# Seven-product FFN pairs that go on adding to sums already read, with a new step order, in a two-layer grid diffusion block on one core

## The chip, the cores and the metric

The kernel runs on one core of a Trainium2 chip. The metric is the device time of one launch in microseconds (us). Inputs and outputs are fp32; TensorE is fed with fp32r operands, and nearly every fp32 product is made of three passes over a high and a low part of each factor, which all add into one PSUM sum.

## The reference

Two layers work on 512 latent tokens and 256 context tokens of width 1024. A layer normalizes and modulates the tokens, projects them, runs four mixers (neighbourhood attention, a gated linear recurrence, retention, differential attention), projects back with `w_out`, and then runs the gated feed-forward part (FFN) on which the change works. The second layer does the FFN on the latent tokens alone:

```python
def swiglu(h, w1, w2):
    g, u = jnp.split(h @ w1, 2, axis=-1)
    return (jax.nn.silu(g) * u) @ w2

h2 = modulate(rms_norm(xl_mid, g_pre_ffn[l]), mod_l[3], mod_l[4])
xl_new = xl_mid + mod_l[5] * rms_norm(swiglu(h2, w_ffn_in[l], w_ffn_out[l]), g_post_ffn[l])
```

`w1` has 2 x 2816 columns: 22 blocks of 128 columns for `g`, and as many for `u`. One block of `g` with the block of `u` that belongs to it is called a pair here.

## The kernel before

Nothing is issued where it is written. Class `Issue` records every operation; its `run` (from line 373) then goes through a list schedule with cost and latency tables, and issues the instructions of each engine in that order, from one line, L573. So all rows of the profile name line 573, and instructions are told apart by tiles: `T` (128 x 1024, 26 of them), `t` (128 x 512, six), `D` (128 x 3072, seven), `st` (small columns), and in PSUM `a` (four of 512 columns) and `s` (two of 1024). What decides the order: the order in which the program is recorded (`ORDER`, a string of letters per layer that says which mixer takes the next step, d, n, l, r, and m for the modulation weights), how far ahead of the oldest open operation a buffer may be taken (`AHEAD`, one number for each of seven stages), a bias between VectorE and ScalarE for operations that either can do (`BIAS`), and limits on the `T` tiles that each use may hold (`LIMIT`). The queues themselves run in order: an instruction that waits holds all behind it on its engine.

The seven stages follow each other with small overlaps: start with the first modulation vectors; mixers of layer 1; `w_out` and FFN pairs of layer 1; the FFN's output product of layer 1; mixers of layer 2; `w_out` and the 22 pairs of layer 2; the output product of layer 2 (`ffn_out8`).

A pair of the second layer is computed in one of two ways. With the halves of the model width and the halves of the tokens it is a 2 x 2 by 2 x 2 block product. `ffn_pair8` (line 1690) makes the eight products of that directly: per product 4 x 3 matmuls of 128 x 128 by 256 columns, 96 in all. `ffn_pair` (line 1629) makes seven (a Strassen-Winograd scheme): 84 matmuls, but more sums on VectorE (DVE), before the products on the weights and after them on the results. The list `CLASSIC` (line 587) names the pairs of each layer that take eight products: in the second layer 0, 1, 2, 14, 18 and 21. In `ffn_pair` each of the seven products has a PSUM region of its own, and the results are put together in `t` tiles.

Other tables that the change touches: `WCH` says in which chunks the eight blocks of `w_out` are taken, for the first and the second half of the tokens; `RES` how many of its split weights stay in SBUF between the halves (two in layer 1, seven in layer 2); `OUT8` how the 22 blocks of `ffn_out8` are grouped; `FIRST` which projection weights are loaded early, among the modulation weights of the start (`prefetch`: index i of the list is loaded with quarter i).

Of the kernel before, what the change touches and what calls it, by code (L numbers as in the profile page):

```python
# [13 lines left out]
AF = mybir.ActivationFunctionType  # L14
ALU = mybir.AluOpType
# [7 lines left out]
NF = DFF // 128  # L23
# [148 lines left out]
class Issue:  # L172
# [7 lines left out]
        def __getattr__(self, fn):  # L180
            return lambda *a, **k: self.q.add(self.name, fn, a, k)

    AHEAD = (10 ** 9, 183, 161, 90, 339, 135, 40)
    LOCK = 1
    BIAS = (100, 800, 500, 0, 200, 300, 200)

    def __init__(self, nc):
        self.real, self.ops, self.tags, self.kinds = nc, [], {}, {}
# [387 lines left out]
class Net:  # L576
# [13 lines left out]
    FIRST = ((3, 0), (7, 0))  # L590
    ORDER = ("drlmddlllrddrrnllrdrmrddrmdrlmrrmmdrdrmdlndmmmddnnnmdmnnnmmdndnnnnnmnnrmnn",
             "dlllldlrdlldrdddrdrrrddrdldnrdnnnnnnnrnrrndnnnrn")

    LIMIT = dict(r=(2, 61, 57, 4, 1, 19, 3), m=(14, 4, 6, 33, 8, 28, 5), wh=(7, 58, 35, 12, 28, 42, 5), fw=(4, 68, 77, 14, 43, 48, 9), fa=(38, 3, 10, 19, 23, 13, 9), W=(20, 43, 11, 9, 28, 32, 41), wo=(97, 51, 25, 30, 33, 17, 9))

    def __init__(self, tc, I, out, ND=7):
        self.tc, self.nc, self.I, self.out = tc, Issue(tc.nc), I, out
# [978 lines left out]
    def ffn_in_T(self, l, halves, ctx, out):  # L1576


        nc = self.nc
        H = 128 * len(halves[0])  # L1580
# [12 lines left out]
        for t, ids in enumerate(halves):  # L1593
            xs = yield
            ns = [self.normed(xs[i]) for i in ids]
            for c in range(0, 8, cpt):
# [16 lines left out]
                nm = "12"[c // 4] + "12"[t]  # L1613
                if nm in names:
                    split(nm, q[t, c], c % 4)
        for c in range(0, 4, cpt):
            b11, b21, b12, b22 = q[0, c], q[0, c + 4], q[1, c], q[1, c + 4]
            t3 = self.T()[:, 0:cpt * H]
            self.sub(t3, b22, b12)
            self.sub(b12, b12, b11)  # L1620
            split("T1", b12, c)
            self.sub(b22, b22, b12)
            split("T2", b22, c)
            self.sub(b21, b22, b21)
            split("T4", b21, c)
            split("T3", t3, c)
        yield

    def ffn_pair(self, l, f, B, dst):
# [57 lines left out]
        nc.scalar.activation(s, s, AF.Silu)  # L1687
        self.tt(dst[:, H:n], s, c22, ALU.mult)

    def ffn_pair8(self, l, f, B, dst):  # L1690

        nc = self.nc
        n = dst.shape[1]
        H = n // 2
        A = [self.split_w(self.raw_in(self.I["w_ffn_in"][l, i])) for i in (f, NF + f)]
        for t in range(2):
            ps = self.S()
            g, u = (ps[:, i * 512:i * 512 + H] for i in range(2))
            for out, (wh, wl) in zip((g, u), A):
                for k in range(8):  # L1700
                    bh, bl = (B["12"[k // 4] + "12"[t], w][:, k % 4 * H:(k % 4 + 1) * H] for w in "hl")
                    c = slice(k * 128, k * 128 + 128)
                    self.mm3(out, wh[:, c], wl[:, c], bh, bl, k == 0, k == 7)
            s = nc.buf("t")[:, 0:H]
            nc.scalar.activation(s, g, AF.Silu)
            nc.vector.tensor_tensor(dst[:, t * H:(t + 1) * H], s, u, ALU.mult)
            if t == 0:
                yield

    def ffn(self, l, B, ctx, order):  # L1710
# [7 lines left out]
        for i, f in enumerate(seq):  # L1718
            if ctx:
                dst[f] = (self.W() if i < NF - self.KEEP else self.T())[:, 0:n]  # L1720
            else:
# [375 lines left out]
```

## Time and profile before

| | |
|---|---|
| median of 3 runs | 1703.21 us (1701.01 to 1704.25) |
| the profiled execution | 1701.83 us |
| its span, first to last instruction | 1700.0 us |
| busy: TensorE, its weight loads, DVE, ScalarE, GpSimd | 96%, 84%, 73%, 49%, 10% |
| mean granted clock of TensorE | 0.982 of full speed |

The profile shows for each engine when it was busy and what ended its idle time; PE is TensorE, PEld its weight loads, ACT is ScalarE, POOL is GpSimd, SP is the engine whose queue starts the transfers. A clock of 1.00 is the 2.4 GHz level, 0.50 the 1.2 GHz level. Instructions of one engine overlap a little at their ends, so that the distance from start to start is a better price for one of a row of them than its own length.

### The profile page before, as it was taken

What the parts mean: (1) busy time and instruction counts of PE and PEld (TensorE: products, weight loads), DVE (VectorE), ACT (ScalarE), POOL (GpSimd) and SP (SyncE); (2) the same over time, 40 slices, a digit from 0 to 9 for tenths busy, and PEclk for the clock granted to TensorE, in tenths of its full rate; (3) what the DMA queues carried; (4) which work ended last, traced back from release to release, by engine and by line L of the source; (5) the groups of instructions that cost most, each with busy time, mean ns of one, the idle gap of its engine ahead of it and who ended that gap; (6) DMA issues with size and microseconds to landing.
All of it is one profiled execution on the core that took longest, in us unless ns stands there. A gap on an engine that the chain in (4) does not pass through costs nothing. (4 is left out here: it accounts for less than half of the span.)

```text
span 1700.0 us, 26804 instructions
## 1 busy us (share of the span) xinstructions
PE 1638.9 (96%) x10487; PEld 1420.5 (84%) x10487; DVE 1248.2 (73%) x2133; ACT 831.3 (49%) x1388; POOL 161.8 (10%) x152
## 2 busy tenths in 40 slices
PE   7998999999999999999999889999999999999998
PEld 4887778677869999999987678889877899999886
DVE  5686656848589877887689998888656799886442
ACT  4366734767564333343343475765555544443221
POOL 1010100000111011001001220022120000100000
PEclk8999999999999999999999989999989999999999
DMA  9342467657573232233955551532134422332332
GB/s 377 115 149 62 162 226 260 214 182 260 187 257 136 69 112 93 101 104 108 313 174 195 207 197 57 186 130 79 38 118 149 173 83 92 112 99 89 118 129 75
DMA packets 81617, 254.64 MB, mean 150 GB/s; under 512 B 8661, under 2 KB 14133, under 8 KB 81489
## 3 DMA queue, kind: packets, MB, share of 16 engines
q1 hardware_dynamic: 81224, 252.81, 42.8%
q8 instruction: 82, 1.34, 0.3%
q14 instruction: 47, 0.38, 0.1%
q10 hardware_dynamic: 264, 0.11, 0.0%
HBM read 224.80 MB, written 28.08 MB: 149 GB/s over the span
## 5 line engine op out<-in xcount | busy, mean ns | idle before, releaser
L573 ACT ACT_TABLE_LOAD x30 | 38.5, 1283 | 7.2 <-issue 2.6
L573 PE MATMUL a<-D_0u,T_21u 128*128 128x384 f32 (+2 forms) x88 | 27.4, 340 | 0.0
L573 PE MATMUL a<-D_0u,T_12u 128*128 128x256 f32 (+2 forms) x84 | 26.4, 337 | 0.0
L573 PE MATMUL a<-D_0u,T_25u 128*128 128x256 f32 (+2 forms) x68 | 23.5, 346 | 0.0
L573 PE MATMUL a<-D_0u,T_1u 128*128 128x256 f32 (+2 forms) x76 | 22.5, 334 | 0.0
L573 PE MATMUL a<-D_0u,T_18u 128*128 128x256 f32 (+2 forms) x64 | 19.4, 335 | 0.1
L573 PE MATMUL s<-D_6u,D_4u 128*128 128x512 f32 (+1 forms) x66 | 17.9, 355 | 1.4 <-issue 1.1
L573 PE MATMUL s<-D_4u,D_5u 128*128 128x512 f32 (+1 forms) x66 | 17.8, 358 | 1.1 <-ACT T_17u L573 0.6
L573 PEld LDWEIGHTS a<-D_0u,T_21u 128*128 128x128 f32 x88 | 16.5, 190 | 2.1 <-DVE T_16u L573 0.9
L573 ACT COPY t_4u<-s 128x384 f32<-128x384 f32 (+1 forms) x16 | 6.9, 430 | 22.2 <-PE s L573 22.1
L573 PE MATMUL a<-D_2u,T_25u 128*128 128x512 f32 (+1 forms) x52 | 17.7, 341 | 0.0
L573 DVE TENSOR_TENSOR st_6u<-st_6u 128x1 f32<-128x1 f32 x1 | 0.2, 159 | 23.7 <-ACT T_15u L573 23.7
L573 PEld LDWEIGHTS s<-D_6u,D_4u 128*128 128x128 f32 x66 | 11.0, 188 | 7.7 <-ACT T_18u L573 1.7
L573 PE MATMUL a<-D_3u,T_12u 128*128 128x384 f32 (+2 forms) x52 | 16.9, 351 | 0.0
L573 ACT COPY t_5u<-s 128x384 f32<-128x384 f32 (+1 forms) x12 | 5.2, 434 | 23.3 <-PE s L573 23.3
L573 PEld LDWEIGHTS a<-D_0u,T_12u 128*128 128x128 f32 x84 | 15.6, 188 | 1.1
L573 PE MATMUL a<-D_0u,T_22u 128*128 128x256 f32 (+2 forms) x48 | 15.0, 328 | 1.6 <-ACT T_25u L573 1.6
L573 PE MATMUL a<-D_3u,T_1u 128*128 128x512 f32 (+2 forms) x52 | 16.4, 341 | 0.0
L573 ACT ACTIVATE t_1u<-t_1u 128x384 f32<-128x384 f32 (+1 forms) x17 | 8.2, 480 | 16.8 <-DVE t_1u L573 16.8
L573 PEld LDWEIGHTS a<-D_0u,T_25u 128*128 128x128 f32 x68 | 12.9, 190 | 4.0 <-issue 1.9
L573 PE MATMUL a<-D_2u,T_12u 128*128 128x256 f32 (+1 forms) x48 | 16.1, 336 | 0.0
L573 PE MATMUL a<-D_3u,T_25u 128*128 128x512 f32 (+2 forms) x48 | 15.8, 342 | 0.0
(4134 smaller groups left out, 6625.5 us busy)
## 6 DMA issues: line engine op xcount, KB each, us to landing
D_4u<-dstk SPq DMA_DIRECT2D x12, 384.0 KB
T_7u<-in_w_mod_dram SPq DMA_DIRECT2D x8, 512.0 KB
T_6u<-in_w_mod_dram SPq DMA_DIRECT2D x7, 512.0 KB
T_20u<-in_w_mod_dram SPq DMA_DIRECT2D x7, 512.0 KB
T_22u<-in_w_in_dram SPq DMA_DIRECT2D x7, 512.0 KB
T_24u<-in_w_mod_dram SPq DMA_DIRECT2D x6, 512.0 KB
T_1u<-in_w_in_dram SPq DMA_DIRECT2D x6, 512.0 KB
D_6u<-dstk SPq DMA_DIRECT2D x8, 384.0 KB
```

The source lines that it names most:

```text
L573: getattr(getattr(self.real, op.eng), fn)(*map(real, a), **{x: real(v) for x, v in k.items()})
```

## The change

Three things change.

First, a new function `ffn_pair_sums` takes the place of `ffn_pair` in the second layer. It makes seven products as well, with 84 matmuls, but in three PSUM tiles x, y and z: a product is read out by a copy or a sum, and the next product is added to what the tile holds (`start=False`), so that sums which DVE made before are made in PSUM. The block T4 of the activations gets the other sign for this. Per pair, DVE's or GpSimd's sums of 128 x 256 go from nine to five, copies out of PSUM from two to three.

Second, pairs 14, 18 and 21 of the second layer go from eight products to seven; 0, 1 and 2 stay at eight.

Third, the tables get new values: `AHEAD`, `BIAS`, `LIMIT`, `ORDER`, `FIRST`, `EARLY`/`FILL`, `WCH`, `RES`, `OUT8`. `FILL` 4 in the place of 22 moves nothing: the four steps that are left to it are taken with pairs 0 to 3 in both. `RES` 1 and 4 means one more load and split of a `w_out` block in layer 1 and three more in layer 2.

```diff
-    AHEAD = (10 ** 9, 183, 161, 90, 339, 135, 40)
+    AHEAD = (703, 192, 161, 90, 368, 120, 10)
-    BIAS = (100, 800, 500, 0, 200, 300, 200)
+    BIAS = (50, 500, 500, 200, 200, 500, 300)
...
-    WCH = (((3, 2, 1, 1, 1), (3, 1, 1, 3)), ((4, 4), (1, 1, 2, 4)))
-    RES = (2, 7)
+    WCH = (((3, 2, 1, 1, 1), (3, 1, 1, 3)), ((5, 3), (4, 4)))
+    RES = (1, 4)
...
-    CLASSIC = ((), (0, 1, 2, 14, 18, 21))
-    OUT8 = (3, 2, 2, 2, 2, 2, 2, 2, 2, 3)
+    CLASSIC = ((), (0, 1, 2))
+    OUT8 = (2, 4, 3, 2, 2, 1, 2, 3, 3)
-    FIRST = ((3, 0), (7, 0))
+    FIRST = ((9, 0),)
...
+        x, y, z = (self.A()[:, 0:H] for _ in range(3))
+        c11, c12, c22 = (nc.buf("t")[:, 0:H] for _ in range(3))
+        product(x, "11", "11")
+        product(y, "12", "21")
+        self.copy(c11, x)
+        add(c11, c11, y, ALU.add)
+        nc.scalar.activation(c11, c11, AF.Silu)
+        yield
...
+        product(x, "S2", "T2", False)
+        self.copy(c12, x)
+        product(z, "S1", "T1")
+        self.copy(c22, z)
+        product(x, "S3", "T3", False)
+        add(c22, c22, x, ALU.add)
+        product(z, "S4", "22", False)
+        add(c12, c12, z, ALU.add)
+        nc.scalar.activation(c12, c12, AF.Silu)
+        self.tt(dst[:, H:n], c12, c22, ALU.mult)
+        product(x, "22", "T4", False)
+        add(dst[:, 0:H], c11, x, ALU.mult)
...
+        seven = self.ffn_pair if ctx else self.ffn_pair_sums
+        jobs = [(self.ffn_pair8 if i in self.CLASSIC[l] else seven)(l, f, B, dst[f]) for i, f in enumerate(seq)]
```

What this does to the order shows at three places.

DVE, in the middle of the second layer's pairs, before, from the operations around one pair to those of the next (`a` and `s` are PSUM results, 512 and 1024 wide rows prepare the weights of a later pair):

```order
L573 TENSOR_TENSOR t_2u_13380<-t_2u_13380,s_81 128x256
L573 TENSOR_TENSOR T_11u_13348<-T_11u_13348 128x512
L573 TENSOR_TENSOR T_20u_13482<-T_13u_13353,T_9u_13464 128x1024
L573 TENSOR_TENSOR t_1u_13498<-t_2u_13380,a_76 128x256
L573 TENSOR_TENSOR T_22u_13503<-T_11u_13348,T_15u_13487 128x1024
L573 TENSOR_TENSOR t_2u_13380<-t_2u_13380,t_5u_13477 128x256
L573 TENSOR_TENSOR T_13u_13518<-T_10u_13445,T_17u_13458 128x1024
L573 TENSOR_TENSOR t_5u_13477<-t_5u_13477,t_1u_13498 128x256
L573 TENSOR_TENSOR t_0u_13535<-T_14u_13451 128x512
L573 TENSOR_TENSOR t_1u_13498<-t_1u_13498,a_78 128x256
L573 TENSOR_TENSOR t_2u_13380<-t_2u_13380,a_77 128x256
```

The same place now, one whole pair:

```order
L573 TENSOR_TENSOR T_9u_13466<-T_24u_13358,T_22u_13431 128x1024
L573 TENSOR_TENSOR t_1u_13473<-t_1u_13473,a_77 128x256
L573 TENSOR_TENSOR t_3u_13452<-t_3u_13452,a_78 128x256
L573 TENSOR_TENSOR T_24u_13519<-T_1u_13475,T_19u_13503 128x1024
L573 TENSOR_TENSOR T_5u_13524<-t_3u_13452,t_1u_13473 128x256
L573 TENSOR_TENSOR T_5u_13524<-t_0u_13415,a_77 128x256
L573 TENSOR_TENSOR t_4u_13533<-T_11u_13480 128x512
L573 TENSOR_TENSOR T_11u_13480<-T_1u_13475,T_11u_13480 128x512
L573 TENSOR_TENSOR T_7u_13552<-t_4u_13533,T_4u_13544 128x512
L573 TENSOR_TENSOR t_5u_13538<-t_5u_13538,a_79 128x256
L573 TENSOR_TENSOR T_1u_13475<-t_4u_13533,T_1u_13475 128x512
L573 TENSOR_TENSOR T_1u_13475<-T_1u_13475 128x512
```

The third 1024 wide subtraction of the pair has gone to GpSimd: in the stage of `w_out` and pairs of the second layer GpSimd now has 21 of that width, four before.

ACT, near the end of the second layer's mixers, before: casts of mixer results that come back from DRAM (`D<-T`), among copies of PSUM tiles that the attention's matmuls wait for:

```order
L573 COPY T_25u_11557<-s_81 128x1024
L573 CAST D_6u_11573<-T_16u_11526 128x512
L573 CAST D_4u_11579<-T_10u_11531 128x512
L573 COPY T_14u_11476<-a_77 128x128
L573 CAST D_4u_11579<-T_13u_11544 128x512
L573 ACTIVATE T_25u_11584<-s_80,kd_1u_9353 128x6x64
L573 COPY T_10u_11603<-s_81 128x1024
```

And now:

```order
L573 COPY T_22u_11561<-s_80 128x1024
L573 ACTIVATE T_19u_11512<-T_19u_11512,st_4u_11544 128x512
L573 CAST D_6u_11573<-T_14u_11528 128x512
L573 COPY T_3u_11478<-a_79 128x128
L573 CAST D_0u_11585<-T_5u_11533 128x512
L573 COPY T_19u_11596<-s_80 128x1024
```

A normalization step (`T_19u`), one cast and a small copy stand before the second cast now, and one operation less before the copy of the `s` tile.

SP, at the start, before: the loads of tokens, then projection weights (`in_w_in`) among the modulation weights:

```order
L573 DMA T_17u_185<-in_w_in_dram 128x1024
L573 DMA T_18u_199<-in_w_mod_dram 128x1024
L573 DMA T_19u_209<-in_w_mod_dram 128x1024
L573 DMA T_22u_226<-in_w_mod_dram 128x1024
L573 DMA T_24u_244<-in_w_mod_dram 128x1024
L573 DMA T_1u_251<-in_w_in_dram 128x1024
L573 DMA T_6u_261<-in_w_mod_dram 128x1024
```

And now:

```order
L573 DMA T_15u_175<-in_w_in_dram 128x1024
L573 DMA T_16u_189<-in_w_mod_dram 128x1024
L573 DMA T_17u_199<-in_w_mod_dram 128x1024
L573 DMA T_20u_216<-in_w_mod_dram 128x1024
L573 DMA T_22u_234<-in_w_mod_dram 128x1024
L573 DMA T_24u_241<-in_w_mod_dram 128x1024
L573 DMA T_1u_251<-in_w_mod_dram 128x1024
```

The second projection weight no longer stands among them, and the eight modulation weights that followed it move one place up. Over all engines, TensorE has 36 matmuls of 256 columns fewer and no other count changed; ACT loads an activation table 26 times in the place of 30. The order of the instructions is new in both mixer stages and in the second layer's `w_out` and pairs. From the end of the first layer's `w_out` to its fourth pair, and from its output product to the first projections of the second layer's mixers, TensorE's order is nearly that of before.

## Rows read from the trace of the kernel before

**Rows 1.** The page, busy us of each engine (share of the span) xinstructions.

```profile
PE 1638.9 (96%) x10487; PEld 1420.5 (84%) x10487; DVE 1248.2 (73%) x2133; ACT 831.3 (49%) x1388; POOL 161.8 (10%) x152
```

**Rows 2.** Windows by stage: length, busy us (xinstructions), granted clock, DMA share, GB/s.

```profile
0.00:43.00 43.00, 30.73 (x391) 20.88 (x391) 21.99 (x68) 21.05 (x43) 5.97 (x24) 0.84 0.97 378
43.00:409.00 366.00, 353.29 (x2539) 275.85 (x2538) 241.34 (x483) 216.79 (x393) 25.80 (x15) 0.99 0.52 181
409.00:825.00 416.00, 409.84 (x2274) 384.16 (x2274) 324.79 (x481) 182.25 (x280) 42.39 (x33) 0.99 0.39 138
825.00:1015.00 190.00, 177.30 (x789) 144.05 (x788) 168.73 (x279) 89.14 (x152) 27.47 (x29) 0.97 0.60 206
1015.00:1295.00 280.00, 274.55 (x1847) 234.19 (x1847) 216.34 (x393) 173.18 (x285) 42.38 (x33) 0.97 0.34 115
1295.00:1337.00 42.00, 42.00 (x192) 34.16 (x191) 25.62 (x39) 16.35 (x31) 2.73 (x5) 1.00 0.30 110
1337.00:1571.00 234.00, 229.95 (x1937) 228.10 (x1936) 197.40 (x323) 108.36 (x170) 12.84 (x9) 1.00 0.33 106
```

**Rows 3.** Windows cut at the stretches with the 1.2 GHz clock, three of eight.

```profile
13.60:27.30 13.70, 8.27 (x77) 4.18 (x78) 8.17 (x20) 7.57 (x13) 3.13 (x5) 0.50 1.02 408
...
1146.90:1153.70 6.80, 6.80 (x39) 6.46 (x39) 4.38 (x8) 2.59 (x4) 4.02 (x2) 0.50 0.03 12
1249.30:1259.50 10.20, 10.20 (x45) 8.54 (x41) 4.63 (x12) 2.01 (x4) 0.00 (x0) 0.50 0.34 103
```

**Rows 4.** A window in the middle of the second layer's pairs.

```profile
1390.00:1420.00 30.00, 30.00 (x258) 30.00 (x257) 28.40 (x51) 15.10 (x24) 0.00 (x0) 1.00 0.30 102
```

**Rows 5.** Timeline of DVE among these pairs: start, us, instruction [idle before <-releaser].

```profile
1403.20 1.23 DVE L573 TENSOR_TENSOR T_9u<-T_5u,T_20u 128x1024 fp32r<-128x1024 f32 x1
1404.34 0.41 DVE L573 TENSOR_TENSOR t_1u<-t_1u,s 128x256 f32<-128x256 f32 x1
```

**Rows 6.** Timeline of PE there: the last matmul of the product read at 1404.34.

```profile
1403.20 0.28 PE L573 MATMUL s<-D_4u,T_22u 128*128 128x256 f32 x1
```

**Rows 7.** Timeline of DVE at 1477 to 1480, with the instruction of Rows 8 beside it.

```profile
1477.72 1.52 DVE L573 TENSOR_TENSOR t_4u<-t_4u,t_1u 128x256 f32<-128x256 f32 x1
1479.17 0.68 DVE L573 TENSOR_TENSOR T_12u<-t_5u,T_12u 128x512 f32<-128x512 f32 x1
1479.77 0.41 DVE L573 TENSOR_TENSOR t_1u<-t_1u,t_2u 128x256 f32<-128x256 f32 x1
```

**Rows 8.** Timeline of POOL at 1477.

```profile
1477.61 1.36 POOL L573 TENSOR_TENSOR T_3u<-t_5u,T_6u 128x512 fp32r<-128x512 f32 x1 [7.82 <-PE s L573]
```

**Rows 9.** Groups of POOL by form, 1337 to 1571: xcount | busy us, mean ns.

```profile
L573 POOL TENSOR_TENSOR T_1u<-T_24u,T_19u 128x1024 fp32r<-128x1024 f32 x1 | 2.4, 2405 | 111.0 <-PE s L573 111.0
```

**Rows 10.** Timeline of DVE at 1482, and of PE right after it.

```profile
1482.28 0.43 DVE L573 TENSOR_TENSOR T_10u<-t_4u,t_1u 128x256 f32<-128x256 f32 x1 [0.49 <-ACT t_4u L573]
1482.62 0.41 DVE L573 TENSOR_TENSOR t_5u<-t_3u,s 128x256 f32<-128x256 f32 x1
...
1483.09 0.39 PE L573 MATMUL s<-D_4u,T_18u 128*128 128x256 f32 x1 [1.12 <-DVE t_5u L573]
```

**Rows 11.** Timeline of ACT at the end of the second layer's mixers.

```profile
1245.33 0.62 ACT L573 CAST D_6u<-T_16u 128x512 fp32r<-128x512 f32 x1 [3.56 <-DMA T_16u<-mixd]
1245.99 0.62 ACT L573 CAST D_4u<-T_10u 128x512 fp32r<-128x512 f32 x1
...
1247.19 0.58 ACT L573 ACTIVATE T_25u<-s,kd_1u 128x384 f32<-128x384 f32 x1
1247.66 1.01 ACT L573 COPY T_10u<-s 128x1024 f32<-128x1024 f32 x1
```

**Rows 12.** Timeline of PE at the same place.

```profile
1248.73 0.66 PE L573 MATMUL a<-T_10u,T_6u 128*64 128x128 f32 x8 [2.01 <-ACT T_10u L573]
```

**Rows 13.** Timeline of SP's queue at the start.

```profile
16.01 0.33 SPq L573 DMA_DIRECT2D T_1u<-in_w_in_dram  x1
17.28 0.33 SPq L573 DMA_DIRECT2D T_6u<-in_w_mod_dram  x1
```

More of the change, by code (lines that the diff above doesn't have):

```diff
@@ L580 @@
     KEEP, LATE, LEAD = 2, 2, 1
-    EARLY, FILL = 8, 22
-    WCH = (((3, 2, 1, 1, 1), (3, 1, 1, 3)), ((4, 4), (1, 1, 2, 4)))
-    RES = (2, 7)
+    EARLY, FILL = 8, 4
+    WCH = (((3, 2, 1, 1, 1), (3, 1, 1, 3)), ((5, 3), (4, 4)))
+    RES = (1, 4)
     HOOK = 10
@@ L586 @@
     NS = 2
-    CLASSIC = ((), (0, 1, 2, 14, 18, 21))
-    OUT8 = (3, 2, 2, 2, 2, 2, 2, 2, 2, 3)
+    CLASSIC = ((), (0, 1, 2))
+    OUT8 = (2, 4, 3, 2, 2, 1, 2, 3, 3)
     QK1 = 'QK'
-    FIRST = ((3, 0), (7, 0))
-    ORDER = ("drlmddlllrddrrnllrdrmrddrmdrlmrrmmdrdrmdlndmmmddnnnmdmnnnmmdndnnnnnmnnrmnn",
-             "dlllldlrdlldrdddrdrrrddrdldnrdnnnnnnnrnrrndnnnrn")
-    LIMIT = dict(r=(2, 61, 57, 4, 1, 19, 3), m=(14, 4, 6, 33, 8, 28, 5), wh=(7, 58, 35, 12, 28, 42, 5), fw=(4, 68, 77, 14, 43, 48, 9), fa=(38, 3, 10, 19, 23, 13, 9), W=(20, 43, 11, 9, 28, 32, 41), wo=(97, 51, 25, 30, 33, 17, 9))
+    FIRST = ((9, 0),)
+    ORDER = ("drlddmlllrddrrnllrdrmrddrmdrlmrrmmdmrdlrdndmmdndmmnmdmnmdndmnnnnnnnnmnrnnn",
+             "dlldlldlrdldlddrmldddrrdrrrdnrdnnnnnnnnrnrrndnnnr")
+    LIMIT = dict(r=(8, 12, 44, 4, 2, 18, 7), m=(43, 6, 6, 2, 17, 35, 12), wh=(24, 16, 19, 16, 21, 19, 5), fw=(28, 37, 9, 19, 4, 18, 30), fa=(31, 13, 5, 9, 30, 42, 39), W=(27, 12, 27, 9, 25, 30, 26), wo=(4, 21, 20, 31, 40, 31, 4))
     def __init__(self, tc, I, out, ND=7):
@@ L652, in sub, with mm3 @@
         self.tt(out, x, y, ALU.subtract, by)
-    def mm3(self, out, lh, ll, rh, rl, start, stop):
+    def mm3(self, out, lh, ll, rh, rl, start, stop, **more):
         mm = self.nc.tensor.matmul
         with self.nc.together():
-            mm(out, lhsT=lh, rhs=rh, start=start, stop=False)
-            mm(out, lhsT=lh, rhs=rl, start=False, stop=False)
-            mm(out, lhsT=ll, rhs=rh, start=False, stop=stop)
+            mm(out, lhsT=lh, rhs=rh, start=start, stop=False, **more)
+            mm(out, lhsT=lh, rhs=rl, start=False, stop=False, **more)
+            mm(out, lhsT=ll, rhs=rh, start=False, stop=stop, **more)
     def bcast_rows(self, ap, n):
@@ L1623, in ffn_in_T @@
             split("T2", b22, c)
-            self.sub(b21, b22, b21)
+            self.sub(b21, *((b22, b21) if ctx else (b21, b22)))
             split("T4", b21, c)
@@ L1688, in ffn_pair, with ffn_pair_sums, split, product @@
         self.tt(dst[:, H:n], s, c22, ALU.mult)
+    def ffn_pair_sums(self, l, f, B, dst):
+        nc = self.nc
+        n = dst.shape[1]
+        H = n // 2
+        g, u = (self.raw_in(self.I["w_ffn_in"][l, i]) for i in (f, NF + f))
+        lo, hi = slice(0, 512), slice(512, 1024)
+        A = {}
+        def split(x, *names):
+            for w, t in zip("hl", self.split_w(x)):
+                for i, nm in enumerate(names):
+                    A[nm, w] = t[:, i * 512:(i + 1) * 512]
+        def product(ps, a, b, first=True):
+            for k in range(4):
+                wh, wl = (A[a, w][:, k * 128:(k + 1) * 128] for w in "hl")
+                bh, bl = (B[b, w][:, k * H:(k + 1) * H] for w in "hl")
+                self.mm3(ps, wh, wl, bh, bl, first and k == 0, k == 3, skip_group_check=not first)
+        add = nc.vector.tensor_tensor
+        split(g, "11", "12")
+        x, y, z = (self.A()[:, 0:H] for _ in range(3))
[6 more added lines that the diff above has]
+        yield
+        s1 = nc.buf("t")
+        self.tt(s1, u[:, lo], u[:, hi], ALU.add)
+        self.sub(u[:, lo], g[:, lo], u[:, lo])
+        self.sub(g[:, lo], s1, g[:, lo])
+        self.sub(g[:, hi], g[:, hi], g[:, lo])
+        split(s1, "S1")
+        split(g, "S2", "S4")
+        split(u, "S3", "22")
+        product(x, "S2", "T2", False)
[10 more added lines that the diff above has]
+        add(dst[:, 0:H], c11, x, ALU.mult)
     def ffn_pair8(self, l, f, B, dst):
@@ L1726, in ffn @@
                 dst[f] = big[:, j % m * n:(j % m + 1) * n]
-        jobs = [(self.ffn_pair8 if i in self.CLASSIC[l] else self.ffn_pair)(l, f, B, dst[f]) for i, f in enumerate(seq)]
+        seven = self.ffn_pair if ctx else self.ffn_pair_sums
+        jobs = [(self.ffn_pair8 if i in self.CLASSIC[l] else seven)(l, f, B, dst[f]) for i, f in enumerate(seq)]
         for job in jobs[:self.LEAD]:
```

## The prediction

> **What bounds the kernel now.** I read the page's busy shares first, then the windows by stage, then those windows in which TensorE is not full. TensorE is busy for 1638.9 of 1700.0 us [rows 1]; all other engines have room over the whole span. By stage [rows 2] the 61.1 idle us lie in few places: 12.3 in the start (43.00 - 30.73), 12.7 in the first layer's mixers, 6.2 in its `w_out` and pairs, 12.7 around its output product (825 to 1015), 5.5 in the second layer's mixers, 4.1 in its pairs, and most of the rest behind the last matmul. The second loss is the clock: in eight stretches the granted clock is 0.50, the 1.2 GHz level, and half of TensorE's busy time in such a stretch is lost [rows 3]: 4.1 us in the first, 3.4 and 5.1 in the two of the second layer's mixers. The reader should see there that the clock falls behind places where TensorE waited: the long one at 1249 stands right behind a wait of 2.01 us at 1248.73 [rows 12].
>
> In the pairs, where the code changes, TensorE is full: 258 matmuls in 30.00 us, 30.00 us busy, clock 1.00 [rows 4]. One matmul of 256 columns costs 0.1163 us there, and one that goes is 0.1163 us less, as long as nothing else gets late. DVE is busy for 28.40 of the same 30.00 us, so it is the engine to ask.
>
> **The change, part by part.** The sum is made on the profiled execution, 1701.83 us. The median is 1703.21, 1.38 more, and I carry that over.
>
> 1. Three pairs from eight products to seven: 3 x (96 - 84) = 36 matmuls, all in a stretch where TensorE is full: 36 x 0.1163 = 4.2 us less.
>
> 2. DVE in the pairs. From start to start, a 1024 wide subtraction takes 1.14 us (1404.34 - 1403.20 [rows 5]), a 512 wide one 0.60 (1479.77 - 1479.17 [rows 7]), a 256 wide sum 0.34 (1482.62 - 1482.28 [rows 10]). A seven-product pair before: 3 x 1.14 + 5 x 0.60 + 9 x 0.34 = 9.5 us, against 84 x 0.1163 = 9.8 us of TensorE. So the eight-product pairs gave DVE time to catch up. With sums made in PSUM and one subtraction moved to GpSimd a pair is 2 x 1.14 + 5 x 0.60 + 5 x 0.34 = 7.0 us. That lets the three pairs change without DVE becoming the bound: nothing from this on the path by itself. The one wait that I can follow to DVE in the middle of the pairs, 1.12 us at 1483.09 (DVE had waited 0.49 us for ScalarE with the sum that TensorE needed queued behind it [rows 10]), stood in a crowded DVE queue; I take it as gone, 1.1 us less; the bounds are 0 and 1.1.
>
> 3. The waits that `ffn_pair_sums` adds. A tile must be read before the next product goes into it. In the new order the next product into the same tile is always another product away: 12 x 0.1163 = 1.40 us. The nearest row for the hand-off: the last matmul of a product starts at 1403.20 and is over at 1403.48 [rows 6]; DVE stands in a 1024 wide subtraction then, and its sum runs from 1404.34 to 1404.75 [rows 5]. That is 1.27 us from the end of the product to the end of the sum, with a full subtraction ahead of it, so it fits into 1.40, by little. A copy on ScalarE has one cast before it and fits as well. Behind a late sum stand TensorE, and on DVE the preparation of the weights of a pair later on. I take 0; the bounds are 0 and a repeat of the 1.12 us wait in every pair, 19 x 1.12 = 21 us.
>
> 4. GpSimd takes 21 subtractions of 1024 in this stage, four before. One lasts 2.40 us [rows 9], and in one pair of 9.8 us there is one. GpSimd is idle otherwise. While GpSimd's 1.36 us subtraction ran [rows 8], a DVE sum with both inputs in SBUF took 1.52 us instead of 0.41 [rows 7]: it was held until GpSimd was done. The Trainium skill states this as a rule (SBUF — State Buffer, Terms): DVE and GpSimd contend for a shared port pair, which is held for a whole instruction while the loser is blocked; rows 7 and 8 agree. So up to 2.40 us of DVE per pair can be blocked, less the two sums on PSUM that the order puts beside it (0.34 each): 7.0 + 2.40 - 0.68 = 8.7 us, still under 9.8. I take 0 here, and make the other case a rival.
>
> 5. `RES` adds four loads and splits of `w_out` blocks. A split is one cast and one subtraction; in 1295 to 1337 DVE is busy for 25.62 of 42 us and ScalarE for 16.35 [rows 2], and the three of layer 2 fall around there: 0. Without that cover the four would cost 4 x 1.14 = 4.6 us of DVE.
>
> 6. The start. One load less stands among the modulation weights; a load takes 1.27 us of the queue (17.28 - 16.01 [rows 13]), so the last eight weights land up to 1.3 us sooner. Against it, TensorE has 27 projection matmuls in the start in the place of 42; 15 that come later are at most 15 x 0.23 = 3.4 us (a matmul of 512 columns at twice 0.1163). I take 0; the bounds are -1.3 and +2.1.
>
> 7. The mixers. Their idle time (12.7 and 5.5 us) and their stretches at 0.50 can be won or lost, since the order is new. I can follow one stall into the new order. ScalarE stands for 3.56 us before a cast whose load is late, and a copy that TensorE waits for ends 3.3 us after that cast began (1248.67 - 1245.33) [rows 11]. In the new order the copy has one cast and one scaling fewer ahead of it, 0.66 (1245.99 - 1245.33) and 0.47 us (1247.66 - 1247.19) from start to start, about 1.1 us. So TensorE's 2.01 us [rows 12] become about 0.9: 1.1 us less. For the rest I have no row that says which way it goes: 0, with bounds from one more stall of this kind per mixer stage, 2 x (2.01 + 5.1) = +14 us, to half of all that is at stake there, some -12 us. Where TensorE's order is nearly that of before (the first layer's `w_out` into its pairs, the output product into the second mixers) the stalls stay: 0.
>
> Sum: -4.2 - 1.1 - 1.1 = -6.4 us: 1701.8 - 6.4 = 1695.4 us for an execution like the profiled one, and 1696.8 beside the median: 1697 us.
>
> **The rivals.**
>
> (a) The mixers gain as well. For it: the stretch of 10.20 us at 0.50 [rows 3] follows a stall that gets shorter, and ACT loads its table four times less. If that stretch stays at full clock, 5.1 us more are won: 1692 us. Against it: the late load is still first in the queue of ScalarE.
>
> (b) The gain is eaten: hand-offs within the pairs wait a little more than the 0.13 us (1.40 - 1.27) that rows 5 and 6 leave, or the start loses its 2.1 us. With 0.22 us per pair, 19 x 0.22 = 4.2, the matmuls saved are paid back: 1701 us, no change that can be told.
>
> (c) Slower: GpSimd's subtraction holds DVE. Place: the 19 pairs of seven products. If DVE reaches an operation with two SBUF inputs just after GpSimd has started, all behind it on DVE is up to 2.40 us late, among it the sum that frees a tile; then 1.0 us per hand-off does not fit into the 0.13 us left, and TensorE waits about 1.1 us as at 1483.09. The saving of 6.4 us is gone from 0.34 us per pair on; at half of the pairs hit, 9.5 x 1.12 = 10.6 us, the time is 1708, and at all of them 1718 us. By the rule of the Trainium skill quoted above this is what must happen where the order does not keep such operations away. For it: the 1.52 us in rows 7. Against it: the new DVE order puts sums on PSUM, which rows 5 to 8 do not show held, around GpSimd's work, and has 1.1 us per pair to spare (9.8 - 8.7).
>
> (d) Slower by new stalls in the mixers: one more like that of 1248 in each of the two mixer stages, 14 us: 1711 us.
>
> **How the numbers follow.** The forecast case, 1693 to 1699, has 0.38; (a), 1682 to 1693, has 0.26; (b), 1700 to 1706, has 0.20; (c) and (d) together 0.16. The prediction is the likeliest, 1697 us, with its own range 1693 to 1700. To leave out no more than 2 in 10 the range reaches to (a) with its further gains and to the half-hit case of (c): 1685 to 1708 us. A measurement of this kernel can tell some 0.2%, 3.4 us, from no change: faster means under 1699.8, slower over 1706.6. Faster: 0.38 + 0.26 = 0.64; same 0.20; slower 0.16.
>
> **What would show it.** Step 1: in the middle of the second layer's pairs TensorE busy for all of a window with about 258 matmuls in 30 us, and the stage from 1337 on some 4 to 5 us shorter. Steps 2 and 4: DVE well under 28.40 of 30.00 us there, and GpSimd with one 2.40 us instruction per pair. Step 3 is wrong if TensorE's waits there name sums or copies of `t` tiles, many times and with some tenths of a microsecond each; rival (c) if they follow DVE operations of over 2 us. Step 7 shows in the windows of the mixers: idle time and granted clock of either stage. The prediction falls if the stages before the pairs change by more than 5 us either way, which rests on no row that I could follow.

## The result, and the profile after

The changed kernel takes 1678.74 us (median of four runs, 1677.18 to 1681.08), the kernel before 1702.11 beside it: a ratio of 0.9873, with a 95% interval from 0.9836 to 0.991. Measured again with other runs the ratio was 0.9868 (0.9844 to 0.9892). So it is some 22 us faster, where 6.4 were forecast and the range reached down to 1685. The profiled execution took 1680.18 us, against 1701.83.

The busy line of its page, which answers to [rows 1]:

```profile
PE 1622.5 (97%) x10451; PEld 1409.6 (84%) x10451; DVE 1233.0 (73%) x2077; ACT 844.5 (50%) x1420; POOL 212.5 (13%) x174
```

TensorE is busy for 16.4 us less with 36 matmuls fewer, and those are worth 4.2. (The other engines' counts changed too, other than the section on the change has it: DVE has 56 instructions fewer, ScalarE 32 and GpSimd 22 more.) The other 12.2 us are the same matmuls at a higher clock. Idle time went from 61.1 to 55.9 us. So of 21.6 us between the two profiled executions 12.2 are clock, 5.2 are waits, and 4.2 are the matmuls that the change is named for.

Windows of the changed kernel, cut at the first matmul of a stage (start; mixers and `w_out` of layer 1; its pairs; output product, mixers and `w_out` of layer 2; its pairs; last product). Columns as in [rows 2]:

```profile
0.00:26.30 26.30, 15.43 (x178) 8.33 (x178) 11.59 (x33) 11.62 (x20) 4.82 (x18) 1.00 0.93 365
26.30:471.50 445.20, 436.09 (x3085) 344.78 (x3082) 304.23 (x595) 253.49 (x468) 33.79 (x33) 1.00 0.54 194
471.50:812.70 341.20, 335.95 (x1941) 325.89 (x1940) 271.50 (x403) 142.20 (x212) 46.20 (x32) 0.99 0.38 133
812.70:1321.00 508.30, 486.88 (x2828) 405.80 (x2827) 417.42 (x713) 286.51 (x474) 74.48 (x64) 0.99 0.43 152
1321.00:1550.80 229.80, 227.08 (x1902) 225.97 (x1901) 173.90 (x264) 125.72 (x205) 49.79 (x24) 0.99 0.33 111
1550.80:1678.40 127.60, 121.02 (x530) 98.85 (x528) 54.41 (x73) 24.96 (x42) 3.39 (x5) 0.99 0.31 103
```

The clock of the first row must not be believed: the clock records of this trace begin at 26 us, and a stretch without a record counts as full. The transposes of 128 columns last 0.42 us there, as in the start of before, where the records show 0.50; at full clock they last 0.27.

Windows in the middle of the pairs (it answers to [rows 4]) and at the four stretches at 0.50 that are recorded, 20.4 us in all (those of before sum to 57.9; three of them are in [rows 3]):

```profile
1370.00:1400.00 30.00, 30.00 (x258) 30.00 (x257) 21.23 (x34) 17.22 (x28) 10.13 (x6) 1.00 0.35 106
...
483.30:486.70 3.40, 3.30 (x16) 2.33 (x20) 3.40 (x6) 2.87 (x8) 0.00 (x0) 0.51 0.23 93
988.50:995.30 6.80, 4.10 (x17) 3.81 (x18) 6.78 (x8) 3.35 (x7) 4.77 (x3) 0.50 0.07 27
1152.40:1155.80 3.40, 3.40 (x28) 2.85 (x27) 2.98 (x3) 0.32 (x2) 1.27 (x1) 0.50 0.35 137
1329.80:1336.60 6.80, 5.97 (x26) 5.58 (x27) 5.95 (x8) 4.85 (x8) 0.00 (x0) 0.50 0.92 372
```

In the pairs TensorE is as full as it was, and DVE has 21.23 of 30.00 us where it had 28.40.

### The profile page after: what moved, and what is told of

It is laid out like the page before. It is cut to its first block, busy times and chain, and to the rows that moved or that the text cites. A ratio compares the mean times of both kernels' runs of the same rounds, so it can differ in the third digit from the quotient of the medians.

```text
span 1678.4 us, 26751 instructions
## 1 busy us (share of the span) xinstructions
PE 1622.5 (97%) x10451; PEld 1409.6 (84%) x10451; DVE 1233.0 (73%) x2077; ACT 844.5 (50%) x1420; POOL 212.5 (13%) x174
## 5 line engine op out<-in xcount | busy, mean ns | idle before, releaser
L573 PE MATMUL a<-D_3u,T_22u 128*128 128x256 f32 (+2 forms) x68 | 21.3, 333 | 0.0
L573 PE MATMUL a<-D_3u,T_19u 128*128 128x256 f32 (+2 forms) x68 | 21.1, 331 | 0.0
L573 PE MATMUL a<-D_0u,T_15u 128*128 128x256 f32 (+2 forms) x72 | 19.5, 313 | 0.0
L573 PE MATMUL a<-D_3u,T_10u 128*128 128x256 f32 (+2 forms) x64 | 19.4, 326 | 0.0
L573 PE MATMUL s<-D_6u,D_4u 128*128 128x512 f32 (+1 forms) x66 | 18.6, 355 | 0.6 <-issue 0.6
L573 PE MATMUL a<-D_3u,T_21u 128*128 128x256 f32 (+2 forms) x60 | 15.9, 302 | 0.0
L573 PE MATMUL a<-D_3u,T_3u 128*128 128x256 f32 (+2 forms) x52 | 15.8, 332 | 0.0
L573 PE MATMUL a<-D_3u,T_11u 128*128 128x256 f32 (+2 forms) x60 | 15.8, 311 | 0.0
L573 PE MATMUL a<-D_0u,T_20u 128*128 128x256 f32 (+2 forms) x52 | 15.5, 326 | 0.0
L573 PE MATMUL a<-D_3u,T_5u 128*128 128x256 f32 (+2 forms) x52 | 15.3, 325 | 0.0
L573 PE MATMUL a<-D_2u,T_15u 128*128 128x256 f32 (+1 forms) x52 | 14.8, 315 | 0.0
```

The source lines that it names most:

```text
L573: getattr(getattr(self.real, op.eng), fn)(*map(real, a), **{x: real(v) for x, v in k.items()})
```

## The experiments

Ratios stand against the kernel before, run on the same chip; its median there was 1702.6, 1706.3, 1702.9 and 1706.3 us in the four groups of runs, so ratios can be compared across groups, and medians cannot.

**1. The kernel before once more (e0_repeat).** No edit.

> The kernel before, once more, with a profile of its own. Three theories for the 21.7 us between the two profiled executions. CLOCK: the new order of the mixers takes away waits of TensorE behind which the clock falls to 0.50; 12.2 us of the gain are matmuls that ran at the half clock, 4.2 are the 36 matmuls, 5.2 are idle time. PAIRS: the new pair function brings most of it. CHANCE: the stretches at 0.50 lie elsewhere from one execution to the next, and the 12.2 us say nothing of the order. CLOCK and PAIRS: the same stretches at 0.50 as in the first profile, within some us (13.6, 160, 235, 491, 976, 1003, 1147, 1249), mean clock 0.982 within 0.002, median 1700 to 1704. CHANCE: stretches at other places, some of them over 100 us away, mean clock off by 0.004 or more.

Measured: ratio 0.9994 (0.9971 to 1.0017), twelve runs from 1694.76 to 1708.32. Windows of its profile at three places:

```profile
120.50:127.30 6.80, 5.85 (x15) 4.69 (x16) 4.02 (x7) 3.59 (x8) 0.00 (x0) 0.50 0.00 0
...
1249.30:1259.50 10.20, 8.59 (x76) 7.34 (x73) 4.34 (x6) 5.95 (x11) 0.00 (x0) 1.00 0.21 80
1349.30:1356.10 6.80, 6.20 (x29) 5.80 (x28) 6.63 (x7) 4.67 (x7) 0.00 (x0) 0.50 0.66 263
```

The stretch of 10.20 us at 1249 [rows 3], on which rival (a) was built, is not there: behind the same wait, 1.61 us this time, the clock stayed at 1.00. In its place there are stretches at 120.5 and 1349. Those of before at 14, 160, 235, 491, 976, 1003 and 1147 came back, up to 8 us later and not all of the same length. So both CLOCK and CHANCE hold in part: a stretch stands behind a wait, but not behind every wait in every execution, and one profile is not enough to price one.

So from here on I compare stages over several profiles. The table gives the length of each stage, cut at the first matmuls as above (the last one ends with the last matmul, 6 to 8 us before the span's end), and from the first instruction to the last matmul TensorE's idle time and half of its busy time in stretches at 0.50. For traces whose records begin at 26, the start is counted as 0.50 from 11.5 on; where it is recorded, the stretch begins between 13.6 and 15.8, so these entries may be some 0.7 us too high.

| | before, twice | e2_pairs | e1_tables, e3_fn6, e12_dve | changed, twice |
|---|---|---|---|---|
| start | 27.0, 27.0 | 26.8 | 26.3, 26.5, 25.7 | 26.3, 26.3 |
| mixers and `w_out`, layer 1 | 453.6, 461.3 | 456.9 | 447.1, 444.9, 447.1 | 445.1, 448.1 |
| pairs, layer 1 | 344.2, 344.6 | 344.2 | 341.7, 341.0, 341.7 | 341.3, 340.8 |
| output product, mixers, `w_out` | 512.4, 506.8 | 509.4 | 507.2, 506.9, 507.4 | 508.3, 506.4 |
| pairs, layer 2, and last product | 355.0, 356.8 | 351.8 | 354.4, 356.1, 350.9 | 350.8, 350.6 |
| idle | 53.3, 56.4 | 61.0 | 51.6, 47.9, 47.8 | 49.4, 48.8 |
| lost to the half clock | 24.6, 25.6 | 16.9 | 9.8, 14.1, 14.1 | 12.8, 14.4 |

By the means of the two executions of each kernel: start -0.7, first mixers -10.9, first pairs -3.4, the middle -2.3, second pairs and last product -5.2, together -22.4 us. In the first mixers and `w_out` TensorE idles for 12.8 and 16.4 us before, 9.1 and 9.4 now, and the half clock costs 5.0 and 9.9 us before, 0.0 and 3.4 now: about half of their 10.9 us each.

**2. Tables alone, pair code alone, and the three pairs (e1_tables, e2_pairs, e3_fn6).** e1 has all new tables with the old pairs, e2 the opposite, e3 undoes only the third part:

```diff
-    CLASSIC = ((), (0, 1, 2))
+    CLASSIC = ((), (0, 1, 2, 14, 18, 21))
```

> All new tables (order, limits, AHEAD, BIAS, WCH, RES, OUT8, FIRST), but the old pair function ffn_pair and eight products in pairs 0, 1, 2, 14, 18 and 21 as before. CLOCK: about -17 us, 1683 to 1688, the stretches at 0.50 in the mixers at 160, 235, 1003 and 1249 gone. PAIRS: -1 to -5 us, 1697 to 1701. If the tables fit the new pair function alone, TensorE waits in the second layer's pairs and the time is over 1690.

> The kernel before with ffn_pair_sums and eight products only in pairs 0, 1 and 2; all tables are the old ones. CLOCK: the 36 matmuls and at most some idle time of the pairs, -4 to -6 us, 1696 to 1698; the mixers' stretches at 0.50 as before. PAIRS: -12 us or more, under 1690.

> The changed kernel, but pairs 14, 18 and 21 of the second layer take eight products again (36 matmuls of 256 columns more). By the forecast's first step +4.2 us: 1682 to 1684. If the three pairs had also brought or cost DVE time that TensorE waits for, +6 or more, or +2 or less.

Measured: e1 0.9891 (0.9859 to 0.9923), 1685.53 us; e2 0.9975 (0.9953 to 0.9997), 1697.79 us; e3 0.9892 (0.9861 to 0.9923), 1684.74 us. PAIRS falls. Of the stretches that were to go in e1, the one at 1003 stayed (at 991.8, 6.8 us). The tables bring 0.0109 x 1702.6 = 18.6 us, the pair code with the three pairs 4.3 (4.9 by the medians). The three pairs alone are 0.9892 - 0.9868 = 0.0024, 4.1 us, the price of 36 matmuls, but from two ratios whose intervals overlap; the profiles say it more sharply: the second layer's pairs last 233.7 us in e3 and 229.8 and 229.5 in the changed kernel.

**3. One layer's tables, order or limits alone (e6_layer1, e8_order, e9_limits, e15_rm).** On the kernel before, e6 takes over only what belongs to the first four stages; e8 only `ORDER` and `FIRST`; e9 all the others; e15, made later, the first layer's `ORDER`, `FIRST`, and two of seven limits, for the first two stages:

```diff
-    LIMIT = dict(r=(2, 61, 57, 4, 1, 19, 3), m=(14, 4, 6, 33, 8, 28, 5), wh=...
+    LIMIT = dict(r=(8, 12, 57, 4, 1, 19, 3), m=(43, 6, 6, 33, 8, 28, 5), wh=...
```

> The kernel before with the new tables of the first layer alone (its ORDER, FIRST, RES and the first four numbers of AHEAD, BIAS and LIMIT); the second layer and all pair code are the old ones. By the stages of the six profiles so far, the first mixers last 382 to 390 us with the old tables and 372 to 374 with the new, its pairs 3 us less, its output product 3 us more. CLOCK (the gain sits in the waits and half clock of the mixers): -8 to -14 us, 1689 to 1695, first mixers 371 to 375 us. If the second layer's mixers bring most: -5 or less.

> The kernel before with the new ORDER strings and FIRST alone; AHEAD, BIAS, LIMIT and the rest are the old ones. ORDER theory (which mixer takes the next step decides where TensorE waits): at least half of the tables' 17 us, 1685 to 1694. LIMIT theory (how far ahead buffers may be taken decides): within 3 us of before, or slower, since old limits and new order do not fit together.

> The kernel before with the new AHEAD, BIAS, LIMIT, WCH, RES and OUT8, but the old ORDER and FIRST. LIMIT theory: at least half of the 17 us, 1685 to 1694. ORDER theory: within 3 us of before, or slower.

> The kernel before with the new ORDER of the first layer, FIRST, and of the limits only r and m (raw weights and modulation weights) of the first two stages. Order alone left the time as it was: in its first mixers TensorE waited 5.7 us for modulation weights. If the limits r and m are what the new order lacked: first mixers 371 to 376 us, 7 us or more less than the kernel before. If it is the other limits or AHEAD: first mixers over 378 us, within 4 us of the kernel before.

Measured: e6 0.9873 (0.9853 to 0.9894), e8 1.0011 (0.9994 to 1.0028), e9 0.9938 (0.9921 to 0.9955), e15 1.0076 (1.0053 to 1.0099). The first layer's tables alone bring 21.7 us, more than I expected and as much as the whole change. Their first mixers and `w_out` last 446.0 us. 4.8 more come from the stages between 812 and 1321: the output product, whose numbers are new, is 2.2 us longer, but the second layer's mixers and `w_out`, whose own tables are the old ones, last 327.8 us where the two executions of before had 337.8 and 332.0. Both of these wait 2.06 us for a GpSimd subtraction at the beginning of these mixers, and e6 does not; the rest I did not follow. Order alone brings nothing, limits alone half, and the order with the two limits that I suspected is 13 us slower. What TensorE waits for in the first mixers shows that a wait removed is replaced by others. The longest group of e8 (us in total, times, longest wait):

```profile
PE a L573 <- DMA T_9u<-in_w_mod_dram: 2.9, 2, 1.8
```

and the longest of e15:

```profile
PE s L573 <- ACT T_3u L573: 6.7, 1, 6.7
```

With the old limits the new order waits for modulation weights, 6.3 us in sum, where the two executions of before wait 2.9 and 2.2; with r and m alone it waits longer for ScalarE, and its first mixers and `w_out` last 475.2 us. Which of the other limits it needs stays open: they were found together, and single ones need not help.

**4. The wait that the new tables take from the first mixers.** The same view of e0_repeat, its mixers and `w_out` of layer 1,

```profile
PE s L573 <- ACT T_17u L573: 4.7, 1, 4.7
PE a L573 <- DMA T_1u<-in_w_mod_dram: 2.2, 2, 1.7
```

and of the changed kernel:

```profile
PE s L573 <- ACT T_16u L573: 1.7, 1, 1.7
PE s L573 <- DVE T_21u L573: 1.1, 1, 1.1
```

`T_17u` and `T_16u` are the same operation, an exponential over an `s` tile that the next matmul into that tile waits for. The timelines tell why it comes earlier. In e0_repeat, GpSimd's subtraction for a projection weight, the two operations of DVE beside it, what ScalarE then waits for, the exponential, and TensorE's matmul (from four answers):

```profile
107.91 2.72 POOL L573 TENSOR_TENSOR T_19u<-T_12u,T_3u 128x1024 fp32r<-128x1024 f32 x1 [87.02 <-ACT T_3u L573]
108.29 2.95 DVE L573 TENSOR_SCALAR T_22u<-T_2u,cols_0u 128x256 f32<-128x256 f32 x2
...
114.45 0.84 ACT L573 CAST T_0u<-T_22u 128x768 fp32r<-128x768 f32 x1 [1.42 <-DVE T_22u L573]
115.91 1.17 ACT L573 COPY t_2u<-a 32x512 f32<-32x512 f32 x2 [0.63 <-DVE T_23u L573]
...
120.41 0.90 ACT L573 ACTIVATE T_17u<-s,st_12u 128x768 f32<-128x768 f32 x1
...
121.45 1.01 PE L573 MATMUL s<-D_4u,D_5u 128*128 128x512 f32 x2 [4.71 <-ACT T_17u L573]
```

In the profile of before that the prediction read, the same place had two shorter waits, 1.84 us at 114.3 and 0.63 at 119.2, and no fall of the clock behind them:

```profile
107.99 0.87 DVE L573 TENSOR_SCALAR T_22u<-T_2u,cols_0u 128x256 f32<-128x256 f32 x2
108.78 5.47 POOL L573 TENSOR_TENSOR T_19u<-T_12u,T_3u 128x1024 fp32r<-128x1024 f32 x1 [87.86 <-ACT T_3u L573]
...
114.31 0.38 PE L573 MATMUL a<-D_0u,T_19u 128*128 128x256 f32 x1 [1.84 <-POOL T_19u L573]
```

It is the hold of [rows 7, 8], and in these profiles the engine that starts second is held. In e0_repeat the weight's cast on ScalarE came at 106.79 and GpSimd was first: DVE's two operations took 2.95 us in the place of 0.87, and ScalarE waited for DVE with the exponential behind in its queue. In before the cast came at 107.65 and DVE was first: GpSimd took 5.47 us in the place of 2.72, and TensorE waited for GpSimd. e2_pairs and e14_before_fill are like e0_repeat there (2.95 and 2.96 us on DVE). In the changed kernel DVE makes that subtraction itself, no GpSimd instruction stands between 100 and 115.7, and the cast that waited for DVE stands behind the exponential (how much either does, I did not separate):

```profile
110.79 1.22 DVE L573 TENSOR_TENSOR T_9u<-T_14u,T_1u 128x1024 fp32r<-128x1024 f32 x1 [1.92 <-ACT T_1u L573]
...
116.98 0.90 ACT L573 ACTIVATE T_16u<-s,st_12u 128x768 f32<-128x768 f32 x1
117.88 0.82 ACT L573 CAST T_20u<-T_11u 128x768 fp32r<-128x768 f32 x1
...
118.03 0.50 PE L573 MATMUL s<-D_4u,D_5u 128*128 128x512 f32 x1 [1.71 <-ACT T_16u L573]
```

So the exponential starts 3.4 us earlier, and TensorE's wait is 3.0 us shorter. With the old tables and the new pair code, or with the new limits and the old order, the wait was 4.64 (e2_pairs) and 5.46 us (e9_limits); as in e0_repeat, a stretch of 6.8 us at 0.50 begins within it.

**5. Does the clock fall because TensorE waits? (e11_fill, e14_before_fill, e13_fill12).** Each adds matmuls whose sums nobody reads in front of a wait, and leaves the order of all else as it is. e11 puts 20 in front of the projection at 989.8, into the tile that this projection then starts afresh:

```diff
         for _, op in order:
...
+            if op.i == 4770:
+                for _ in range(20):
+                    self.real.tensor.matmul(real(op.a[0][1][0])[:, 0:128], lhsT=ident, rhs=ident, start=True, stop=True)
```

e14 puts 16 in front of the wait of 4.7 us in the kernel before, e13 in front of twelve waits of the changed kernel, both into an `a` tile that is free at that point. The timelines show each of these fp32 matmuls twice (x40 and x32).

> The changed kernel with 20 matmuls of 128 x 128 by 128 fp32 columns added ahead of the first projection of the second mixers, where TensorE waits 5.11 us (984.7 to 989.8) and the clock then is 0.50 for 6.8 us (988.5 to 995.3, in all profiles of old and new tables alike); their sums are overwritten, and the order of all other instructions is the same. If the wait of TensorE is what the clock falls for: no stretch at 0.50 between 980 and 1000, 0 to 3.4 us less in all. If the clock falls there for another reason: the stretch stays, and the time is the same within 1 us or up to 4 us more.

> The kernel before with 16 such matmuls (3.7 us) in front of one wait in the first mixers, where TensorE waits for the exponential that frees an s tile (4.71 us at 121.45 in the second profile of the kernel before, 4.64 at 120.96 with the new pair code, with 6.8 us at 0.50 behind both; in the first profile the wait was split, 1.84 at 114.3 and 0.63 at 119.2, and the clock stayed). If the clock falls for the wait: no stretch at 0.50 between 105 and 135, and 0 to 4 us less. If it falls for another reason: a stretch there, and up to 4 us more.

> The changed kernel with matmuls that do nothing (fp32, 128 x 128 by 128 columns, 0.23 us each, into a PSUM tile that is free) in front of twelve waits of TensorE, two thirds to nine tenths as long as the wait in the profile: 11 before the wait of 3.20 us at 483, 10 before that of 2.89 at 962, 27 before the two of 5.11 and 1.41 at 989.8, two to five before nine shorter ones in the mixers and behind the second w_out; the order of all else is the same. If the clock falls for TensorE's waits: at most two stretches at 0.50 left between 30 and 1670 (five to seven in the profiles of the changed kernel), and 3 to 8 us less, 1671 to 1677. If the waits only shift, so that the matmuls added come on top: 1680 or more.

Measured: e11 0.9845 (0.9825 to 0.9866), 1677.32 us against 1680.54 for the changed kernel in the same group of runs; e14 0.9979 (0.9963 to 0.9996); e13 0.984 (0.9815 to 0.9865). First the changed kernel without filling, in its second profile, then e11: the timeline of TensorE, and windows behind the wait.

```profile
992.41 0.58 PE L573 MATMUL a<-T_7u,D_3u 128*128 128x256 f32 x1 [5.11 <-ACT T_7u L573]
```

```profile
992.10:998.80 6.70, 4.97 (x21) 4.68 (x22) 6.38 (x7) 3.23 (x5) 4.35 (x3) 0.50 0.20 76
```

```profile
985.63 4.63 PE L576 MATMUL a<-ident_0u 128*128 128x128 f32 x40
990.91 0.38 PE L578 MATMUL a<-T_7u,D_3u 128*128 128x256 f32 x1 [0.65 <-ACT T_7u L578]
992.91 0.39 PE L578 MATMUL a<-T_24u,D_3u 128*128 128x256 f32 x1 [1.62 <-DVE T_24u L578]
```

```profile
990.20:993.50 3.30, 1.03 (x7) 0.78 (x7) 3.30 (x5) 1.60 (x2) 3.30 (x2) 1.00 0.00 0
993.50:996.90 3.40, 3.40 (x19) 3.40 (x18) 3.07 (x5) 1.64 (x3) 1.16 (x2) 0.50 0.26 106
```

The projection starts 5.51 us after the start of the last matmul of the stage before in both (986.90 and 985.40), but its 256 columns take 0.38 us and not 0.58, and the stretch at 0.50 is half as long and begins behind the next wait, of 1.62 us, which was not filled. Halving the stretch is worth 1.7 us at most, so the 3.2 us between the medians, whose ratios have overlapping intervals, are not shown to be the filling's alone. e14, TensorE's timeline at the filled wait and the window behind it:

```profile
116.95 3.84 PE L584 MATMUL a<-ident_0u 128*128 128x128 f32 x32 [0.41 <-ACT t_2u L586]
121.27 0.61 PE L586 MATMUL s<-D_4u,D_5u 128*128 128x512 f32 x2 [0.48 <-ACT T_17u L586]
```

```profile
121.00:135.00 14.00, 13.73 (x105) 12.27 (x106) 11.85 (x20) 9.54 (x21) 0.00 (x0) 1.00 0.00 1
```

And e13, everything between the start and the end of the last product:

```profile
26.40:1670.00 1643.60, 1618.82 (x10433) 1412.75 (x10431) 1219.49 (x2039) 831.86 (x1400) 206.51 (x155) 1.00 0.44 150
```

There is no stretch at 0.50 left in its 1644 us. Its ratio is 0.0028 under the second one of the changed kernel, about 4.8 us. Among the versions here e11 and e13 are the fastest by ratio, but the intervals overlap with that of the changed kernel. The runs do not show that filling makes the time steadier: the four of e13 lie within 1.6 us, but so do nearly the four of e12 (1.7), where nothing is filled. The Trainium skill (TensorE: Matmul & The Clock Gate, HAM oscillation) puts a clock that falls again and again down to waits for data between bursts of matmuls. These three runs agree, and the filled waits show that it is the missing matmuls, not what they wait for.

**6. All pairs with seven products; the second layer's tables; GpSimd (e4_all7, e10_best, e12_dve).** e4 sets `CLASSIC` to `((), ())`; e10 is the changed kernel with the old numbers for the last three stages, the second `ORDER`, `WCH`, `RES` and `OUT8`; e12 lets DVE alone make the subtractions that split the weights of the second layer's seven-product pairs (GpSimd has 17 instructions fewer).

> The changed kernel with seven products in all 22 pairs of the second layer (36 matmuls of 256 columns fewer than the changed kernel). If TensorE stays full in the first three pairs too: -4.2 us, 1673 to 1676. If DVE, which still has the splits of w_out and the normed halves there, cannot prepare three more weights by sums: TensorE waits in the first pairs, 1678 or more.

> The first layer's new tables, the new pair function with eight products in pairs 0, 1 and 2, but the old tables for the second layer (ORDER, AHEAD, BIAS, LIMIT, WCH, RES, OUT8). The first layer's tables alone gave the ratio 0.9873, the pair code on the old tables -4.9 us. If the second layer's new tables bring nothing of their own: 0.9873 - 4.9/1702 = 0.9844, 2 to 5 us under the changed kernel. If they are needed for the new pairs or save waits in the second mixers: 3 us or more over the changed kernel.

> The changed kernel with the 1024 wide subtractions of the second layer's pairs on DVE alone; GpSimd takes none of them. By the forecast's fourth step GpSimd's hold on DVE costs nothing, and DVE at 7.0 + 1.1 = 8.1 us per pair stays under TensorE's 9.8: within 2 us of the changed kernel. Rival (c) (GpSimd holds DVE and TensorE waits for it): 3 us or more faster. If DVE has no room: slower by 3 us or more.

Measured: e4 0.9918 (0.99 to 0.9937), e10 0.9862 (0.9841 to 0.9884), e12 0.986 (0.9836 to 0.9884), the changed kernel 0.9868 beside the last two. What TensorE waits for in the pairs of e4:

```profile
PE a L573 <- ACT D_1u L573: 8.2, 1, 8.2
PE a L573 <- DVE T_6u L573: 5.3, 1, 5.3
```

e4 is 8.5 us slower than the changed kernel, and its second pairs last 242.4 us in the place of 229.8. The first pairs overlap the end of `w_out`. With seven products they need more of the activations and sums on weights at once, and DVE is busy for 29.48 of 32 us there: the eight products in pairs 0 to 2 are worth their 36 matmuls. e10 is as fast as the changed kernel: the second layer's tables bring nothing of their own that can be told, and the three splits of `w_out` that the second layer makes again (`RES`) cost nothing that can be told. But for that case I had expected e10 to be 2 to 5 us faster than the changed kernel, and it is not: on top of the first layer's tables the pair code brings 0.9873 - 0.9862 = 0.0011, 1.9 us, where it brought 4.3 on the old ones. The intervals allow both. e12 shows, within what the intervals allow, that it does not matter who subtracts.

## Why the prediction was wrong

**Step 1 was right:** 4.2 us forecast, 4.1 measured by e3_fn6, and 3.9 to 4.2 by the length of the pairs. **Steps 2 to 4 held:** in the changed kernel's pairs no wait of TensorE is left between 1340 and 1550, so the hand-offs fit into their 1.40 us and the stall of [rows 10] has no successor; pair code and three pairs bring 4.3 to 4.9 us, with 5.3 forecast. GpSimd's hold on DVE, rival (c), is there, and it is not rare. Beside 8 of GpSimd's 20 wide subtractions between 1350 and 1550 an operation of DVE with its inputs in SBUF is stretched: six products 256 wide to between 0.88 and 1.16 us (the 14 others of their kind in the window, with nothing on GpSimd beside them, take 0.41 to 0.43), one subtraction 512 wide to 2.28 (0.69 alone), one 1024 wide to 3.06 (1.22 alone). One of the six, with what ran beside it:

```profile
1500.50 2.41 POOL L573 TENSOR_TENSOR T_15u<-T_23u,T_12u 128x1024 fp32r<-128x1024 f32 x1 [7.46 <-PE a L573]
1501.84 0.42 DVE L573 TENSOR_TENSOR T_25u<-t_0u,a 128x256 f32<-128x256 f32 x1 [0.99 <-PE a L573]
1502.18 1.02 DVE L573 TENSOR_TENSOR T_25u<-t_5u,t_1u 128x256 f32<-128x256 f32 x1
```

The sum on PSUM is not held, the product of two tiles in SBUF is, until GpSimd ends at 1502.91; and no wait of TensorE follows. The Trainium skill's rule on the shared port pair (SBUF — State Buffer, Terms) agrees with these rows. So rival (c) had the hold right and its price wrong: DVE had the room that step 4 gave it. **Step 5 held** as far as e10_best shows it (the three splits of the second layer), and **step 6** was off by 0.7 us, within its bounds.

**Step 7 failed.** The stall that it followed went as it said: 2.01 us [rows 12], 0.9 forecast, and now

```profile
1232.62 0.62 ACT L573 CAST D_6u<-T_14u 128x512 fp32r<-128x512 f32 x1 [1.56 <-DMA T_14u<-mixd]
...
1233.82 1.01 ACT L573 COPY T_19u<-s 128x1024 f32<-128x1024 f32 x1
...
1234.89 0.66 PE L573 MATMUL a<-T_19u,T_7u 128*64 128x128 f32 x8 [0.73 <-ACT T_19u L573]
```

The copy ends 2.21 us after the late cast began, where it was 3.34: the 1.1 us that were forecast. That TensorE's wait came out so near is partly luck. With the old order at this place the same wait was 2.01, 1.61 (e0_repeat) and 1.05 us (e14_before_fill), and it is 0.63 in e6_layer1, whose copy ends 3.34 us after the cast as before.

What failed is all around it. First, "for the rest I have no row that says which way it goes: 0": the first mixers (with `w_out`) gave 10.9 us and the middle stages 2.3, together more than the bound of 12. That bound was also too low for what it names: idle time and half clock in the two mixer windows of the first profile were 18.2 and 13.5 us, and half of that is 16. The sign that the prediction gave for its own fall, more than 5 us in the stages before the pairs, came: 17 us. The wait of 4.7 us that went was not to be seen at that size in the one profile that I read, and its stretch at 0.50 not at all; whether it is whole hangs there on which of DVE and GpSimd starts first. Second, the first layer's pairs, 3.4 us shorter, had no term of their own; the step looked only at their beginning. In them e0_repeat waits

```profile
PE s L573 <- ACT T_7u L573: 3.1, 1, 3.1
PE s L573 <- DVE t_5u L573: 1.3, 1, 1.3
...
PE s L573 <- DVE t_1u L573: 0.6, 1, 0.6
PE s L573 <- DVE t_3u L573: 0.5, 1, 0.5
```

and the changed kernel

```profile
PE s L573 <- ACT T_6u L573: 3.2, 1, 3.2
PE a L573 <- DVE D_5u L573: 1.2, 1, 1.2
```

The three waits for sums in `t` tiles (2.4 us, in the middle of the stage) are gone. It is the limits that take them away, with the other numbers that e9 sets, and not the order: in e9_limits they are gone and the stage lasts 340.6 us, in e8_order they are there and it lasts 344.7. The hand-over into the pairs, the first row, stayed as forecast. Third, the clock: I priced it by the stretches of one execution, and gave the one at 1249 to a rival of its own. That one comes and goes without any change. What counts is how many waits a kernel has behind which the clock can fall: in the table the half clock costs 17 to 26 us with the old tables and 10 to 14 with the new ones.

So rival (a), the mixers gain as well, was right in kind, with a wrong place and a third of the size: 5.1 us on top of the forecast, where the stages outside the second pairs gave some 16 more than the 1.1 of step 7. That e6_layer1 alone reaches the ratio of the whole change says where the change was: not in the new function, but in the numbers that order the first layer.

## What to carry to other kernels

Price a wait of TensorE with the half clock that can follow it, and look at several profiles of the same kernel before pricing a stretch: a wait that is split in one execution can be whole, and cost twice as much, in the next. Where it comes and goes, look at what ran beside the engine that is waited for: here it was GpSimd beside DVE. Where a new order touches a stage, give that stage bounds from all of its idle time and all of its half clock, also where TensorE's own order is unchanged. A wait that can't be removed can be filled with matmuls that nobody reads, which takes back the clock and not the wait.

## What the hardware showed beyond the expected

Which of DVE and GpSimd was held changed between two executions of one program, with a start that moved by less than 1 us: 2.95 us on DVE in the place of 0.87, or 5.47 us on GpSimd in the place of 2.72. A wait of 1.61 us left the clock at 1.00 (e0_repeat, 1254.7), and one of 2.01 us at the same place was followed by 10.20 us at 0.50 [rows 3, 12]. With twelve waits filled (e13_fill12), 1644 us passed without one such stretch, and in the three other runs of that kernel the mean clock was 0.993 to 0.998. The mean clock of a profile is no measure across kernels: its records began between 10 and 27 us from the first instruction, and what lies before them counts as full speed.
